# Seven instead of four SwiGLU pairs computed by seven products, in a Conformer / RG-LRU block on one core

## The chip, the cores and the metric

The kernel runs on one core of a Trainium2 chip. Five engines work side by side and meet through semaphores: TensorE (PE in the profile, with its weight loads as PEld), VectorE (DVE), ScalarE (ACT), GpSimd (POOL) and SyncE (SP), which here issues every DMA transfer. The metric is the time of one execution on the device, in microseconds (us); lower is better. All inputs and the output are float32, and the matmuls take them as pairs of fp32r parts, a high part and the low part that is left over.

## What is computed

The block has a token mixer (a causal Conformer convolution beside an RG-LRU recurrence, merged by gates), then a SwiGLU channel mixer, with a residual and an RMSNorm around each. Sequence 512, width 1024, channel mixer 2816 wide. The change sits in the channel mixer:

```python
def reference(x, norm1_g, w_in, ...):
    ...
    m = jax.nn.sigmoid(z_ga) * y_a + jax.nn.sigmoid(z_gb) * y_b
    x = x + m @ w_mix_out[l]

    h = rmsnorm(x, norm2_g[l])
    x = x + (jax.nn.silu(h @ ffn_w1[l]) * (h @ ffn_w3[l])) @ ffn_w2[l]
    return rmsnorm(x, norm_f_g)
```

## The kernel before

**Stages.** By their matmuls in the trace: the way in (`z`, `g`: 0 to 325 us), the two ways out of the token mixers (`yb` with the chunks `lo`, 325 to 380; `ya` with the chunks `co`, 380 to 423), the mixers' merged product (`mxr`, to 463), the SwiGLU products (`f` and `fr`, 463 to 700) and the last product with `ffn_w2` (`or`, 700 to 803).

**Products.** Every product is three matmuls: high by high, high by low, low by high. A SwiGLU *pair* is the two tiles k and k + 11 of 128 hidden columns each (KF = 11 pairs); the plain form (`mm3`, L432, called at L1063 and L1064) takes 2 tiles x 2 weights x 8 blocks x 3 = 96 matmuls of 512 columns. A pair in `SEVEN` (L44) goes through `ffn_seven` (L1011): seven quarter products, Strassen's scheme in Winograd's form, of 2 x 4 x 3 = 24 matmuls of 256 columns each, 168 in all, with sums of the inputs (`f_inputs`, L990, made once) and of the weights. Plain before: pairs 0, 1 and 6 to 10; seven products: 2 to 5.

**Sums of weights for the SwiGLU pairs.** `make_f_sums` (L315) is a generator; `next(f_sums_steps, None)` runs one step of it per entry of `ORDER` (64 entries, L764) and per tile of `yb` (8, L791). Each pair has four pieces. A piece loads 2 x 256 KB into a tile of the pool `wsums` (3 tiles, L87), two steps later does four additions on GpSimd (L342 to L345), and five weight chunks after that stores 512 KB (L349) to DRAM, from where the chunks `ft..` fetch it again. A piece starts every third step, from step 4.

**Weight chunks.** `weights(key)` (L161) emits the chunks up to four ahead. A chunk takes a tile of the pool `raws` (4 tiles, L85) and one DMA of 512 KB or two of 256 KB, then a tile of `hls` (5 tiles, L86): ScalarE copies the high part (L117) and VectorE, or GpSimd in the way in, subtracts for the low part (L118). A plain pair has four chunks (`raw_f`), a pair of seven products has seven (three `raw_fb`, four `raw_ft`). The last product has chunks of two quarters, in the order b21_0, b11_0, b11_1, b21_2, b11_2, b11_3, b21_4, ... (L249 to L255); b11_k also holds t1 of k and is used from step k on, b21_k serves steps k and k + 1.

**Sums of the weights of the last product.** `out_sums(n)` (L959) makes the next n of eleven: `make_sums` (L276) takes two `raws` tiles, loads 512 KB into each (L279), does four VectorE operations, and stores 4 x 256 KB (L289) to DRAM. The code calls it behind each pair: 2 behind a plain pair, `k % 2` behind one of seven products, and whatever is left behind pair 10 (L1066). Before, this gives 2, 0, 1, 0, 1, 2, 2, 2, and 1 behind pair 9: none is left behind pair 10.

**Sums of a pair's results.** `Sevenfold.pair` (L825) makes the operands of the last product from a finished pair's tiles: 6 VectorE operations (one of 0.69 us, five of 0.42) and two ScalarE casts. It is called as soon as the pair is done (L823, L1054). It leaves five of the 63 `long` tiles (L32) in use per pair until the last product.

**Order.** Instructions of one engine run in order. A scheduler fixes that order when the kernel is built: of the instructions that could go, the earliest in the program first; an instruction that needs a pool tile goes when one is free. `tc.issue_after` adds lower bounds only.

Of the kernel before, what the change touches and what calls it, by code (L numbers as in the profile page):

```python
# [9 lines left out]
F32R = mybir.dt.float32r  # L10
# [3 lines left out]
P = 128  # L14
T = 512
# [25 lines left out]

SEVEN = (2, 3, 4, 5)  # L44
SUMS_AT, SUMS_STEP, SUMS_LAG, STORE_LAG = 4, 3, 2, 5


# [33 lines left out]
def tile_block(ctx, tc, a, out):  # L81
    nc = tc.nc
    pool = lambda name, bufs, **k: ctx.enter_context(tc.tile_pool(name=name, bufs=bufs, **k))
    consts = pool("consts", 1)
    raws = pool("raws", RAW)  # L85
    hls = pool("hls", HL)  # L86
    wsums = pool("wsums", 3)  # L87
    psum = pool("psum", 6, space=bass.MemoryType.PSUM)
    psum2 = pool("psum2", 2, space=bass.MemoryType.PSUM)

# [6 lines left out]
    def pairt(name, dtype=F32R):  # L97

        return longt(f"{name}h", dtype), longt(f"{name}l", dtype)
# [7 lines left out]
    vec, act, pe, pool_e = nc.vector, nc.scalar, nc.tensor, nc.gpsimd  # L107
# [4 lines left out]
    def sub(eng, o, x, y):  # L112
        return eng.tensor_tensor(out=o, in0=x, in1=y, op=ALU.subtract)  # L113

    def split_to(h, l, full, eng, copy=act.copy):

        copy(h, full)  # L117
        last = sub(eng, l, full, h.bitcast(F32))  # L118
        if eng is pool_e:
            newest["sub"] = last.ins  # L120
        return h, l

    def split(name, full, eng, p_=None, copy=act.copy):
        p_ = p_ or pairt(name)
        return split_to(*p_, full, eng, copy)
# [4 lines left out]
    emitted = [0]  # L130
# [70 lines left out]
    ORDER = """u0 u1 rx0 rx1 gb0 rx2 u2 g0 rx3 gb1 g1 u3 rx4 g2 gb2 r0 r1 u4 g3 rx5 rg0 g4 rx6 rg1 u5 r2 r3 g5 rx7  # L201
        gb3 rg2 rx8 g6 rg3 u6 r4 r5 rx9 g7 gb4 rg4 u7 g8 r6 r7 rg5 gb5 g9 rg6 gb6 r8 r9 rg7 gb7 ga0 rg8 ga1 rg9
        ga2 ga3 ga4 ga5 ga6 ga7""".split()
    ORDER = [(t.rstrip("0123456789"), int(t.lstrip("abcdefghijklmnopqrstuvwxyz"))) for t in ORDER]
# [92 lines left out]
    F_SUMS = ("t2", "t1", "t4", "t3")  # L297
    f_sums = {k: dram.tile([P, 4, 1024], F32, tag=f"fs{k}", name=f"fs{k}") for k in SEVEN}

# [15 lines left out]
    def make_f_sums():  # L315

        todo = [(k, i, c) for k in SEVEN for i in range(2) for c in (0, 2)]
        sums_due, stores_due = [], []  # L320
        n = 0
        while todo or sums_due or stores_due:
            if stores_due and emitted[0] >= stores_due[0][0]:
                stores_due.pop(0)[1]()
            if sums_due and n >= sums_due[0][0]:
                sums_due.pop(0)[1]()
            if todo and n >= SUMS_AT and (n - SUMS_AT) % SUMS_STEP == 0:
                k, i, c = todo.pop(0)
                raw = wsums.tile([P, 1024], F32, tag="wsum", name=f"fws{k}_{i}_{c}")
                q = [raw[:, 256 * m : 256 * m + 256] for m in range(4)]  # L330
                four = (w1, w3)[i].rearrange("p (h k) (e n) -> p h k e n", h=2, e=2)
                with tc.issue_after(newest["load"]):
                    for h in range(2):
                        nc.sync.dma_start(
                            raw[:, h * T : h * T + T].rearrange("p (e k n) -> p e k n", e=2, k=2),
                            four[:, h, c : c + 2, :, k * P : (k + 1) * P].rearrange("p k e n -> p e k n"),
                        )

                def sums(raw=raw, q=q, k=k, at=T * i + P * c):
                    q11, q12, q21, q22 = q  # L340
                    with tc.issue_after(newest["sub"]):
                        sub(pool_e, q22, q22, q12)  # L342
                        sub(pool_e, q12, q12, q11)
                        pool_e.tensor_tensor(out=q11, in0=q22, in1=q11, op=ALU.add)
                        sub(pool_e, q21, q21, q11)  # L345

                    def stores():
                        with tc.issue_after(newest["load"]):
                            nc.sync.dma_start(f_sums[k][:, :, at : at + 256], raw.rearrange("p (m n) -> p m n", m=4))  # L349

                    stores_due.append((emitted[0] + STORE_LAG, stores))

                sums_due.append((n + SUMS_LAG, sums))
            n += 1
            yield

    for k in range(KF):
        if k in SEVEN:
            for n in ("b11", "b21", "b22", "t2", "t1", "t3", "t4"):
# [84 lines left out]
    def w_tiles(key, kt, ahead=AHEAD):  # L444
        h, l = weights(key, ahead)
        return [(h[:, k, :], l[:, k, :]) for k in range(kt)]
# [205 lines left out]
    def run_beside(n):  # L652
        for _ in range(n):
            next(side, None)
# [107 lines left out]
    f_sums_steps = make_f_sums()  # L762
# [30 lines left out]
            mixq.make_sums(j // 2 - 1)  # L793
    yb = sgb
    run_beside(1000)
    for _ in f_sums_steps:
        pass


    add = lambda o, x, y: vec.tensor_tensor(out=o, in0=x, in1=y, op=ALU.add)  # L800
# [8 lines left out]

    class Sevenfold:  # L810
        def __init__(self, q):
            self.q, self.uv, self.ops = q, [], []
            self.name, self.kh = q.name, q.kh

        def tile(self, j, make):

            k, i = j % self.kh, j // self.kh
            if i == 0:
                self.uv.append((longt(f"{self.name}u{k}"), longt(f"{self.name}v{k}")))
            for dst, cs in zip(self.uv[k], HALVES):  # L820
                make(cs, dst[:, HALVES[i]])
            if i:
                self.pair(k, *self.uv[k])  # L823

        def pair(self, k, ua, va):  # L825

            n = self.name
            u_ = split(f"{n}us{k}", ua, vec)
            s1 = shortt(f"{n}s1{k}")[:, LO]
            add(s1, va[:, LO], va[:, HI])  # L830
            sp = longt(f"{n}s1p{k}", F32R)
            split_to(sp[:, LO], sp[:, HI], s1, vec)
            e = longt(f"{n}e{k}")
            sub(vec, e[:, HI], ua[:, LO], va[:, LO])
            sub(vec, va[:, LO], s1, ua[:, LO])
            sub(vec, e[:, LO], ua[:, HI], va[:, LO])
            self.ops.append((u_, sp, e, va))
# [58 lines left out]
    for n, j in enumerate(mixq.order()):  # L896
        ws = w_tiles(f"co{j}", ND)
        ps = bank(f"ya{j}")
        mm3(ps, ws, un)
        o = sga[j]  # L900
        vec.scalar_tensor_tensor(out=o, in0=ps, scalar=pc("conv_b_out", j), in1=o, op0=ALU.add, op1=ALU.mult)
        m7.tile(j, lambda cs, dst: add(dst, o[:, cs], yb[j][:, cs]))
        if n == 0:
            mixq.make_sums(3)


    x2 = [[longt(f"x2{t}{h}") for h in range(2)] for t in range(NT)]
# [48 lines left out]
    o7 = Sevenfold(outq)  # L956
# [54 lines left out]
    def ffn_seven(k):  # L1011
        u_, v_ = longt(f"ou{k}"), longt(f"ov{k}")

        def product(ps, x_, w_, again=False):

            h, l = weights(f"f{w_}_{k}")
            for i in range(2):
                for c, (xh, xl) in enumerate(f_in[x_]):
                    for m, (lw, rx_) in enumerate(((h, xh), (h, xl), (l, xh))):
                        pe.matmul(  # L1020
                            ps[:, HALVES[i]], lw[:, 4 * i + c, :], rx_, start=not (again or i or c or m),
                            stop=bool(i and c == 3 and m == 2), skip_group_check=True,
                        )

        def out_of(c, dst):
            act.activation(c[:, LO], c[:, LO], AF.Silu)
            vec.tensor_tensor(out=dst, in0=c[:, LO], in1=c[:, HI], op=ALU.mult)

        r1, r2, r3, r5, r7 = bank(f"fr1_{k}"), bank2(f"fr2_{k}"), bank(f"fr3_{k}"), bank2(f"fr5_{k}"), bank(f"fr7_{k}")
        product(r1, "a11", "b11")  # L1030
        c11 = shortt(f"c11_{k}")
        act.copy(c11, r1)
        product(r2, "a12", "b21")
        add(c11, r2, c11)
        out_of(c11, u_[:, LO])
        product(r3, "s4", "b22")
        product(r1, "s2", "t2", True)
        q = shortt(f"q_{k}")
        act.copy(q, r1)
        product(r5, "s1", "t1")  # L1040
        add(q, r5, q)
        c12 = shortt(f"c12_{k}")
        add(c12, r3, q)
        out_of(c12, u_[:, HI])
        product(r7, "s3", "t3")
        c21 = shortt(f"c21_{k}")
        act.copy(c21, r7)
        add(q, r7, q)
        out_of(q, v_[:, HI])
        product(r1, "a22", "t4", True)  # L1050
        add(c21, r1, c21)
        out_of(c21, v_[:, LO])
        o7.uv.append((u_, v_))
        o7.pair(k, u_, v_)  # L1054

    for k in range(1, KF):
        if k in SEVEN:
            ffn_seven(k)
            out_sums(k % 2)
            continue  # L1060
        for j in (k, k + KF):
            p1, p3 = bank(f"f1_{j}"), bank(f"f3_{j}")
            mm3(p1, w_tiles(f"f1_{j}", ND), h2)  # L1063
            mm3(p3, w_tiles(f"f3_{j}", ND), h2)  # L1064
            ffn_out(j, p1, p3)
        out_sums(2 if k < KF - 1 else KF)  # L1066
# [96 lines left out]
```

## Time and profile before

| What | us |
|---|---|
| time, median of 3 runs (lowest, highest) | 814.71 (814.35, 815.43) |
| profiled execution: its time | 814.89 |
| profiled execution: span from first to last instruction | 813.0 |
| DVE busy | 644.1 (79%) |
| ACT busy | 443.1 (55%) |
| POOL busy | 210.3 (26%), nothing between 304 and 476 us |
| one piece of SwiGLU weight sums on POOL (fws) | 4 x 0.74 to 0.76 |
| one sum for the last product on DVE (ows) | 4 x 0.69 |

The profile comes from one execution. Its span is shorter than the time by 1.9 us, which lie around the instructions. A line of the timeline reads: start, duration, engine and line of the code, operation, what it writes and reads, how many merged into this line, and in brackets the idle time before it and what ended that. A line of the windows reads: the stretch, its length, the busy time of each engine with its number of instructions, the granted TensorE clock, the mean busy share of the 16 DMA engines, and what they moved in GB/s.

### The profile page before, as it was taken

The page shows a single profiled execution, that of the slowest core. Times are in us where ns is not written, and L with a number is a line of the kernel's source. Part 1 is how long each engine was busy: PE and PEld are TensorE (multiplying, and loading weights), DVE is VectorE, ACT ScalarE, POOL GpSimd, SP SyncE. Part 2 cuts the span into 40 slices and gives each one's busy share as a digit, 9 for nine tenths or more (in the row PEclk, how much of TensorE's full clock was granted, in tenths as well). Part 3 has the DMA queues.
Part 4 walks back from the last instruction along what each step waited for, and adds up shares of the span by engine and source line. Part 5 has one row for each costly group of instructions (what it writes and reads, how often), then busy time and mean ns, then how long its engine had stood idle before and what let it go on. Part 6 is the DMA issues. An engine that isn't in the chain of part 4 may idle for free.

```text
span 813.0 us, 11453 instructions
## 1 busy us (share of the span) xinstructions
PE 800.0 (98%) x4038; PEld 683.3 (84%) x4038; DVE 644.1 (79%) x1010; ACT 443.1 (55%) x626; POOL 210.3 (26%) x156
## 2 busy tenths in 40 slices
PE   8999999999999999999999999999999999999996
PEld 7988888888887888888888898999988888888884
DVE  4699899998999987777878769797875664688456
ACT  7546688776687755653336554364632223476442
POOL 3565768766675740000000042000000000000000
PEclk9999999999999999999999999999999999999998
DMA  6646475666654522358638535788778778576542
GB/s 209 193 123 171 136 202 176 189 193 198 186 170 130 182 75 65 116 171 263 217 104 259 156 97 176 238 262 248 224 247 282 249 271 297 177 250 216 169 160 104
DMA packets 182029, 153.46 MB, mean 189 GB/s; under 512 B 12519, under 2 KB 150163, under 8 KB 181971
## 3 DMA queue, kind: packets, MB, share of 16 engines
q1 hardware_dynamic: 181971, 152.72, 60.7%
q8 instruction: 32, 0.52, 0.3%
q14 instruction: 26, 0.21, 0.1%
HBM read 123.46 MB, written 26.21 MB: 184 GB/s over the span
## 4 chain that ended last, share of the span: by engine, by line
PE 93%; DVE 4%; issue 1%; DMA 1%; SPq 0%; POOL 0%; ACT 0%; POOLq 0%
PE z L441 31%; PE f L441 19%; PE or L844 13%; PE fr L1020 10%; PE yb L441 7%; PE ya L441 5%; PE mxr L844 5%; DVE cv L600 2%; PE g L721 2%; DMA raw_in<-in_w_in_dram 1%; PE th L481 0%; DVE xb L745 0%; PE tx L481 0%; DVE of L1086 0%; SPq L397 0%
## 5 line engine op out<-in xcount | busy, mean ns | idle before, releaser
L600 DVE SCALAR_TENSOR_TENSOR cv<-u,par,cv 128x511 f32<-128x511 f32 (+17 forms) x240 | 162.6, 729 | 1.1 <-ACT cv L597 0.9
L113 POOL TENSOR_TENSOR hl_in<-raw_in,hl_in 128x1024 fp32r<-128x1024 f32 x52 | 125.5, 2418 | 94.0 <-ACT hl_in L117 92.0
L117 ACT CAST hl_in<-raw_in 128x1024 fp32r<-128x1024 f32 x52 | 54.3, 1044 | 5.9 <-PE z L441 3.0
L117 ACT CAST hl_f<-raw_f 128x1024 fp32r<-128x1024 f32 x28 | 29.3, 1050 | 49.1 <-DMA raw_f<-in_ffn_w_dram 36.0
L113 DVE TENSOR_TENSOR hl_ob<-raw_ob,hl_ob 128x1024 fp32r<-128x1024 f32 (+1 forms) x23 | 27.1, 1178 | 26.8 <-ACT hl_ob L117 26.6
L113 DVE TENSOR_TENSOR hl_f<-raw_f,hl_f 128x1024 fp32r<-128x1024 f32 x28 | 36.2, 1304 | 14.3 <-ACT hl_f L117 14.2
L994 POOL TENSOR_TENSOR hf<-h20h,h20l 128x512 f32<-128x512 f32 x1 | 1.3, 1287 | 171.8 <-DVE h20l L485 171.8
L117 ACT CAST hl_ob<-raw_ob 128x1024 fp32r<-128x1024 f32 (+1 forms) x23 | 23.4, 1015 | 40.3 <-PE or L844 17.4
L441 PE MATMUL z<-h10h,hl_in 128*128 128x512 f32 (+1 forms) x112 | 42.4, 380 | 2.7 <-DVE h10l L485 1.5
L441 PE MATMUL z<-h15h,hl_in 128*128 128x512 f32 (+1 forms) x112 | 42.0, 376 | 0.0
L441 PE MATMUL z<-h16h,hl_in 128*128 128x512 f32 (+1 forms) x112 | 42.0, 376 | 0.0
L441 PE MATMUL z<-h17h,hl_in 128*128 128x512 f32 (+1 forms) x112 | 41.9, 376 | 0.0
L441 PE MATMUL z<-h11h,hl_in 128*128 128x512 f32 (+1 forms) x112 | 41.8, 375 | 0.0
L441 PE MATMUL z<-h12h,hl_in 128*128 128x512 f32 (+1 forms) x112 | 41.8, 375 | 0.0
L441 PE MATMUL z<-h14h,hl_in 128*128 128x512 f32 (+1 forms) x112 | 41.8, 375 | 0.0
L441 PE MATMUL z<-h13h,hl_in 128*128 128x512 f32 (+1 forms) x112 | 41.8, 375 | 0.0
L113 POOL TENSOR_TENSOR fws<-fws 128x256 f32<-128x256 f32 x48 | 36.3, 756 | 2.3
L113 DVE TENSOR_TENSOR ows<-ows,ows 128x512 f32<-128x512 f32 x22 | 15.2, 689 | 20.6 <-DMA ows<-in_ffn_w_dram 20.4
L113 DVE TENSOR_TENSOR hl_ot<-raw_ot,hl_ot 128x1024 fp32r<-128x1024 f32 (+1 forms) x17 | 20.1, 1191 | 11.1 <-ACT hl_ot L117 10.7
L441 PEld LDWEIGHTS z<-h10h,hl_in 128*128 128x128 f32 x112 | 21.3, 191 | 7.4 <-DVE h10l L485 1.8
L117 ACT CAST hl_ot<-raw_ot 128x1024 fp32r<-128x1024 f32 (+1 forms) x17 | 17.5, 1028 | 16.5 <-PE or L844 14.8
L441 PEld LDWEIGHTS z<-h15h,hl_in 128*128 128x128 f32 x112 | 21.4, 191 | 3.8
(905 smaller groups left out, 2574.9 us busy)
## 6 DMA issues: line engine op xcount, KB each, us to landing
raw_in<-in_w_in_dram SPq DMA_DIRECT2D x52, 512.0 KB
raw_f<-in_ffn_w_dram SPq DMA_DIRECT2D x28, 512.0 KB
ows<-in_ffn_w_dram SPq DMA_DIRECT2D x22, 512.0 KB
ot<-ows SPq DMA_DIRECT2D x44, 256.0 KB
raw_ob<-in_ffn_w_dram SPq DMA_DIRECT2D x33, 256.0 KB
raw_ot<-ot SPq DMA_DIRECT2D x33, 256.0 KB
fws<-in_ffn_w_dram SPq DMA_DIRECT2D x32, 256.0 KB
fs<-fws SPq DMA_DIRECT2D x16, 512.0 KB
```

Of the source, the lines that this page charges most:

```text
L113: return eng.tensor_tensor(out=o, in0=x, in1=y, op=ALU.subtract)
L117: copy(h, full)
L441: pe.matmul(ps, l, r, start=i == 0, stop=i == n - 1)
L600: vec.scalar_tensor_tensor(out=acc[c][:, s:], in0=u[c][:, : T - s], scalar=dw(c, s), in1=acc[c][:, s:], op0=ALU.mult, op1=ALU.add)
L721: pe.matmul(ps, l, r, start=k == 0, stop=k == len(mms) - 1)
L844: pe.matmul(banks[i], l_[:, ts], r_, start=start and n == 0, stop=stop and n == 2, skip_group_check=again)
L994: pool_e.tensor_tensor(out=v, in0=h2p[c][0].bitcast(F32), in1=h2p[c][1].bitcast(F32), op=ALU.add)
L1020: pe.matmul(ps[:, HALVES[i]], lw[:, 4 * i + c, :], rx_, start=not (again or i or c or m), stop=bool(i and c == 3 and m == 2), skip_group_c ...
```

## The change

It puts pairs 2 to 8 instead of 2 to 5 through seven products, so that 28 instead of 16 pieces of weight sums are made. Pieces start every third step up to step 64 and every second step after; the eight tiles of `ya` now run steps too, and what is left is run behind them. With nothing else due, stores no longer wait for five chunks. A finished pair is put on a list (`waiting`); `release` makes its sums. In a pair of seven products the list is released in its middle, ahead of its sixth product, except for the newest `max(0, k - 6)` pairs: pair 6 waits through pair 7, pairs 6 and 7 through pair 8, and all three are released at the head of pair 9, which is plain. The high and low parts of `us` of pairs 0 to 2 are put into tiles of `wsums` (six `long` tiles less). The calls of `out_sums` are unchanged, and give, from pair 1 on: 2, 0, 1, 0, 1, 0, 1, 0, 2, and 4 behind pair 10.

```diff
-SEVEN = (2, 3, 4, 5)
+PIECES = 3
+SEVEN = (2, 3, 4, 5, 6, 7, 8)
...
-    wsums = pool("wsums", 3)
+    wsums = pool("wsums", PIECES)
...
-        n = 0
+        n, next_at = 0, SUMS_AT
         while todo or sums_due or stores_due:
-            if stores_due and emitted[0] >= stores_due[0][0]:
+            if stores_due and (emitted[0] >= stores_due[0][0] or not (todo or sums_due)):
                 stores_due.pop(0)[1]()
             if sums_due and n >= sums_due[0][0]:
                 sums_due.pop(0)[1]()
-            if todo and n >= SUMS_AT and (n - SUMS_AT) % SUMS_STEP == 0:
+            if todo and n >= next_at:
+                next_at += SUMS_STEP if n < len(ORDER) else SUMS_STEP - 1
                 k, i, c = todo.pop(0)
...
     run_beside(1000)
-    for _ in f_sums_steps:
-        pass
...
             if i:
-                self.pair(k, *self.uv[k])
+                self.waiting.append((k, *self.uv[k]))
+                self.release()
+
+        def release(self, keep=0):
+
+            while len(self.waiting) > keep:
+                self.pair(*self.waiting.pop(0))
 
         def pair(self, k, ua, va):
 
             n = self.name
-            u_ = split(f"{n}us{k}", ua, vec)
+
+            p_ = None
+            if n == "o" and k < PIECES:
+                both = wsums.tile([P, 1024], F32R, tag="wsum", name=f"{n}us{k}")
+                p_ = both[:, :T], both[:, T:]
+            u_ = split(f"{n}us{k}", ua, vec, p_)
...
         if n == 0:
             mixq.make_sums(3)
+        next(f_sums_steps, None)
+
+    for _ in f_sums_steps:
+        pass
...
         out_of(c12, u_[:, HI])
+
+        o7.release(max(0, k - 6))
         product(r7, "s3", "t3")
...
         o7.uv.append((u_, v_))
-        o7.pair(k, u_, v_)
+        o7.waiting.append((k, u_, v_))
 
     for k in range(1, KF):
         if k in SEVEN:
             ffn_seven(k)
             out_sums(k % 2)
             continue
+        o7.release()
         for j in (k, k + KF):
```

More of the change, by code (lines that the diff above doesn't have):

```diff
@@ L811, in __init__ @@
         def __init__(self, q):
-            self.q, self.uv, self.ops = q, [], []
+            self.q, self.uv, self.ops, self.waiting = q, [], [], []
             self.name, self.kh = q.name, q.kh
```

## The prediction

> **What bounds the kernel now.** I read the page's busy times first, then the chain of waits, then the stages as windows, then the DMA issues of SP. The busy times and the chain, merged by line:
>
> ```profile
> PE 800.0 (98%) x4038; PEld 683.3 (84%) x4038; DVE 644.1 (79%) x1010; ACT 443.1 (55%) x626; POOL 210.3 (26%) x156
> ...
> 510.94 80.63 PE fr L1020 x672
> 591.57 108.83 PE f L441 x480
> 700.40 102.93 PE or L844 x453
> ```
>
> TensorE is the bound, and in these three stages without a gap. So only fewer or shorter matmuls gain, and anything that starves PE there costs in full. The stretch of 80.63 us is four pairs by seven products, 20.16 us each; that of 108.83 us is five plain pairs, 21.77 us each. A 256-column matmul takes 80.63 / 672 = 0.120 us, slightly more than half of a plain one's 108.83 / 480 = 0.227.
>
> The windows (the two ways out, one pair by seven products, two plain pairs, the start of the last product):
>
> ```profile
> 314.00:380.00 66.00, 66.00 (x292) 54.64 (x291) 51.36 (x73) 36.53 (x55) 0.00 (x0) 1.00 0.48 152
> 380.00:423.50 43.50, 43.50 (x193) 36.05 (x192) 33.71 (x58) 14.02 (x18) 0.00 (x0) 1.00 0.58 184
> ...
> 531.10:551.30 20.20, 20.20 (x170) 20.20 (x170) 17.71 (x27) 12.91 (x20) 0.00 (x0) 1.00 0.82 249
> ...
> 656.90:678.60 21.70, 21.70 (x97) 17.96 (x97) 12.80 (x22) 6.12 (x8) 0.00 (x0) 1.00 0.85 279
> 678.60:700.40 21.80, 21.80 (x98) 18.06 (x97) 10.61 (x17) 6.01 (x8) 0.00 (x0) 1.00 0.61 212
> 700.40:725.00 24.60, 24.60 (x110) 20.36 (x110) 19.74 (x28) 16.42 (x23) 0.00 (x0) 1.00 0.75 266
> ```
>
> DVE and DMA, not POOL, are what has little left: DVE 17.7 of 20.2 us in a pair by seven products, DMA 279 GB/s at a share of 0.85 in a plain pair with two sums for the last product. The granted clock is 1.00 throughout.
>
> Last, SP's transfers around the plain pairs:
>
> ```profile
> 599.29 1.01 SPq L144 DMA_DIRECT2D raw_f<-in_ffn_w_dram  x2
> 600.40 5.51 SPq L279 DMA_DIRECT2D ows<-in_ffn_w_dram  x3
> 608.27 2.50 SPq L289 DMA_DIRECT2D ot<-ows  x4
> 611.58 0.33 SPq L279 DMA_DIRECT2D ows<-in_ffn_w_dram  x1
> 612.01 1.01 SPq L144 DMA_DIRECT2D raw_f<-in_ffn_w_dram  x2
> 615.98 5.07 SPq L289 DMA_DIRECT2D ot<-ows  x4
> 621.89 1.01 SPq L144 DMA_DIRECT2D raw_f<-in_ffn_w_dram  x2
> 623.00 5.47 SPq L279 DMA_DIRECT2D ows<-in_ffn_w_dram  x3
> ...
> 703.72 3.70 SPq L1076 DMA_DIRECT2D x2b<-x2k  x8
> ```
>
> The order is the program's: the four chunks of the next pair, then the two sums (four loads) of this one, then four chunks again. Nothing later overtakes, since all of them want one of the four `raws` tiles. A sum keeps its two tiles from its load to the landing of its stores: first load at 600.4, next load in a freed tile at 611.6, so 11.2 us, two sums at a time.
>
> **The change, part by part.**
>
> *Three pairs by seven products.* 288 matmuls at 0.227 go, 504 at 0.120 come: 3 x (21.77 - 20.16) = 4.8 us less on PE. This is all there is to win.
>
> *Their chunks and VectorE work.* Seven instead of four 512 KB chunks per pair. Over seven pairs that is 7 x 3.67 MB + 3 sums x 2.10 MB = 32.0 MB in 141.1 us, 227 GB/s, against (4 x 3.67 + 2 x 2.10) / 80.63 = 234 before; the same for DVE, as a sum falls on every second pair as now. PE had no gap there. 0 us, between 0 and 3 (a gap of about 1 us a new pair if a chunk were late).
>
> *Pairs' sums in the middle of the next pair.* The same 2.8 us of DVE (0.69 + 5 x 0.42) and two casts on ACT, moved behind another operation; needed only by the last product. Queued behind them on DVE are the seven products' own additions, whose banks PE wants back a pair later. 0 us; without that cover 2.8 us for each of four pairs. Pairs 6 to 8 come at the head of pair 9: 3 x 2.8 = 8.4 us on a DVE that has 21.8 - 12.8 = 9.0 us idle there. It fits just; it can delay the sums below by some us.
>
> *Twelve more pieces of weight sums.* 12 x 4 x 0.74 = 36 us on POOL, which idles from 304 to 476 us, and 12 x 1.05 MB of transfers; four pieces fall before step 64, the others into the ways out. There 8 x 1.05 = 8.4 MB over 109.5 us raise 165 GB/s (mean of the two windows) to 241, under the 279 shown. On SP, chunks of `lo` and `co` stand behind a store that waits for POOL; `hl_co` is ready some 15 us ahead of PE (third chunk cast at 380.6 for a use at 396.2). 0 us, at most 2 (below).
>
> *The `us` parts in `wsums`, stores not waiting.* Pool bookkeeping; 0 us: the pieces' tiles are free long before pair 0 ends at 490 us. A late store would hold pair 0's sums, wanted only at the last product, 200 us later.
>
> *Four sums behind pair 10.* Here the calls of `out_sums` give 2, 0, 1, 0, 1, 0, 1, 0, 2 and 4, so eight loads of 512 KB stand behind the chunks b21_0, b11_0, b11_1, b21_2 and ahead of b11_2. New times: pair 9 begins at 510.9 + 7 x 20.16 = 652.0, pair 10 at 673.8, the last product at 695.6, and its step 2, which opens with b11_2, 2 x 4.08 us later (steps begin at 700.2 and 704.3 in the matmuls' rows), at 703.7. The four sums begin where the second plain pair's did, 623.0 - 591.6 = 31.4 us after the first plain pair begins: 683.4. Four raw tiles, two sums at a time: 683.4 + 2 x 11.2 = 705.8 is when b11_2 can be loaded. From load to the end of the split a chunk takes 6.3 us (load 599.3, cast 603.2, subtraction to 605.6): ready at 712.1, **8.4 us late**. Lower end: from the buffers alone, were all `raws` and `hls` kept full, the sums' loads start some 1.4 us earlier: 7.0. Upper end, by transfers: three sums and the loads of the fourth are 7.34 MB, at 279 GB/s 26.3 us, chunk ready at 683.4 + 26.3 + 6.3 = 716.0, 12.3 late; if the eight `x2b` and the two `gf` transfers (2.62 MB, 9.4 us) also go ahead of it, 21.7. They went 3.3 us into this stage before, so some of them may. I take the middle of 8.4 and 12.3, **10.4 us**, as tile turnover and transfers are both near their limits in these rows; later chunks come after it in the same order and are not later still.
>
> On this term the Trainium skill, in DMA: Bandwidth & Descriptors (Bandwidth), has 341 GB/s for a 1 MB transfer into SBUF from another issuer; by it the 7.34 MB take an estimated 21.5 us, turnover would bind alone, and the sum would have 8.4 in place of 10.4. No slice of this trace moves more than 282.
>
> **Sum.** -4.8 + 10.4 = +5.6 us: span 813.0 + 5.6 = 818.6; on the median of the runs (0.2 below the profiled 814.89) 814.7 + 5.6 = **820.3**.
>
> **The rivals.**
>
> *Not slower: the sums are out of the way in time.* If b11_2 is loaded by 697.4 (703.7 - 6.3), all of the 4.8 stays: 809.9. For it: chunks are loaded 20 us and more ahead in the plain stretch, and with no sums behind pairs 6 and 8 by seven products the queue may run further ahead than I reckon. Against it: the queue's lead is capped by 4 + 5 tiles, and chunks b11_1 and b21_2 themselves hold `raws` tiles until PE frees `hls`. It decides at a load of b11_2 at 702.2, where the stall equals the gain. Chance 0.20.
>
> *Stall about equal to the gain*, 3 to 6.4 us: 813 to 816.3. Chance 0.06.
>
> *The residual's reload goes first* and its 9.4 us come on top: 21.7 late, 814.7 - 4.8 + 21.7 = 831.6. For it: `long` tiles are freed earlier than before (six fewer used), and these loads need no `raws` tile. Against: part of them overlaps the turnover's idle transfers. Chance 0.10.
>
> *GpSimd slows VectorE in the ways out*, with no late stall. This pair of rows shows it; the first subtraction takes 2.23 us beside GpSimd's additions, against a median of 1.22:
>
> ```profile
> 483.06 2.23 DVE L113 TENSOR_TENSOR hl_f<-raw_f,hl_f 128x1024 fp32r<-128x1024 f32 x1
> ...
> 481.95 2.27 POOL L994 TENSOR_TENSOR hf<-h25h,h25l 128x512 f32<-128x512 f32 x1
> ```
>
> If each of 16 POOL operations held DVE for its 0.74 us in `ya`'s 43.5 us, that were 11.8 us against 9.8 idle: 2 us late, 809.9 + 2 = 811.9. Against: the first chunks' 15 us of lead. The Trainium skill, SBUF — State Buffer, has the two engines take a shared port pair as an exclusive lock for a whole instruction; the two rows agree. Chance 0.04.
>
> *Forecast*: 0.60, own range 816.9 (7.0 late) to 822.2 (12.3 late), with b11_3 and b21_4 late by a little more up to 826.
>
> **How the numbers follow.** Faster or slower means by more than 0.2%, 1.6 us, about what a measurement of this kernel can tell from no change. Slower: 0.60 + 0.10 and nearly none of the second rival: 0.70. Faster: 0.20 + 0.04, less 0.01: 0.23. Same: 0.07. The range has to reach over the not-slower case: 809.5 to 826.0; it leaves out the reload case and little else.
>
> **What would show it.** Right: `fr` with 1176 matmuls in 141 us without a gap, 192 `f` matmuls in 43.5 us, and then, within 10 us of the last product's start, PE idle some 10 us, released by the subtraction of `hl_ob`, with SP showing eight `ows` loads between the loads of b21_2 and b11_2, the last of them near 700. POOL busy to about 440 us. Wrong: no idle PE behind the first two steps of `or` (then the order or the lead was misread, and about 810 comes out), or gaps in `fr` or `ya` instead.

## The result: slower by 2.4%, and the profile after

The changed kernel takes 833.91 us (median of 4 runs, 833.16 to 835.55) against 814.53 us of the kernel before on the same chip (813.86 to 815.43): a ratio of 1.0243, interval 1.0227 to 1.0258 (ratios compare all runs, not the two medians, so they differ a little from the medians' quotient). The forecast was 820.3, its range 809.5 to 826.0. The profiled execution took 835.55 us, its span 833.8, so the spans differ by 20.8 us.

The page's busy times and queue, then the same queue before (its columns: packets, MB moved, share of the time of 16 DMA engines):

```profile
PE 801.6 (96%) x4254; PEld 692.2 (83%) x4254; DVE 674.8 (81%) x1034; ACT 458.3 (55%) x650; POOL 252.2 (30%) x204
...
q1 hardware_dynamic: 199731, 170.03, 66.0%
```

```profile
q1 hardware_dynamic: 181971, 152.72, 60.7%
```

PE is busy about as long as before (801.6 against 800.0 us), although 4.8 us of matmuls are gone: some of its matmuls became slower. The change moves 17.3 MB more: 12 pieces of 1.05 MB, and three more chunks of 0.52 MB for each of three pairs.

Where the 20.8 us are, by the first and last matmuls of each stage:

| Term, by the forecast's names | forecast, us | measured, us |
|---|---|---|
| three pairs by seven products | -4.8 | -4.8 (first `fr` to first `or`: 189.5, now 184.7) |
| chunks, VectorE work and moved sums in these pairs | 0 | 0 |
| twelve more pieces of weight sums (start of `fr`) | 0, at most 2 | +2.2 (510.8, now 513.0) |
| four sums behind pair 10, wait for b11_2 | +10.4 (7.0 to 12.3) | +11.1 |
| later chunks | 0 | +7.1, wait for b21_4 |
| matmuls at a lower granted clock behind these waits | not named | +5.6 |
| the end | 0 | -0.4 |
| sum | +5.6 | +20.8 |

The three terms around `or` make 23.8 us: 103.1 us before, 126.9 now, from its first matmul to the end of the 453rd of its 462, where the chain of waits leaves PE. The windows after (the second way out; the mixers' product; all pairs by seven products; two plain pairs; the starved stretch of the last product), in the columns of before:

```profile
380.00:423.50 43.50, 43.50 (x194) 36.03 (x193) 39.82 (x59) 15.51 (x20) 11.91 (x13) 1.00 0.87 271
423.50:463.00 39.50, 37.72 (x168) 30.37 (x167) 34.72 (x56) 20.69 (x35) 3.11 (x4) 1.00 0.85 270
513.00:654.10 141.10, 141.10 (x1178) 141.10 (x1177) 109.60 (x159) 74.50 (x107) 0.00 (x0) 1.00 0.77 240
654.10:697.60 43.50, 43.50 (x194) 36.02 (x193) 30.54 (x55) 15.80 (x24) 0.00 (x0) 1.00 0.68 222
705.00:736.00 31.00, 12.76 (x44) 9.00 (x43) 17.60 (x28) 9.87 (x15) 0.00 (x0) 0.74 0.91 321
```

The seven pairs run without a gap, 141.1 us of 141.1. The second way out, where some of the pieces went, rose from 184 to 271 GB/s without a gap; PE lost 1.8 us in the mixers' product behind it. That product takes 42.6 us from its first matmul to the first of `f`, against 39.9 before; it began 0.5 earlier, which leaves the 2.2 of the table. In 705 to 736 PE works 12.8 of 31 us while the transfers run at 321 GB/s, share 0.91: the stage waits for data.

PE's waits in the last product (total us, times, longest), and its timeline around the two gaps:

```profile
PE or L855 <- ACT hl_ob L118: 18.2, 2, 11.1
```

```profile
719.76 1.22 PE L855 MATMUL or<-hl_ob,ous 128*128 128x512 f32 x2 [11.11 <-ACT hl_ob L118]
...
734.43 2.91 PE L855 MATMUL or<-hl_ob,ous4h 128*128 128x512 f32 x5 [7.09 <-ACT hl_ob L118]
...
739.27 0.63 PE L855 MATMUL or<-hl_ob,ous4h 128*128 128x512 f32 x1
739.70 0.63 PE L855 MATMUL or<-hl_ob,ous4l 128*128 128x512 f32 x1
...
742.22 0.39 PE L855 MATMUL or<-hl_ob,ous5l 128*128 128x512 f32 x1
742.45 0.62 PE L855 MATMUL or<-hl_ob,ous5h 128*128 128x512 f32 x2
```

Two gaps, both ended by the cast of a chunk of `ffn_w2`: step 2 waits for b11_2, step 4 for b21_4. Behind the second a matmul starts every 0.43 us (739.27, 739.70), later every 0.23 (742.22, 742.45).

What SP sends in that time:

```profile
686.27 0.81 SPq L243 DMA_DIRECT2D raw_ob<-in_ffn_w_dram  x2
687.17 5.62 SPq L280 DMA_DIRECT2D ows<-in_ffn_w_dram  x3
...
699.47 1.33 SPq L280 DMA_DIRECT2D ows<-in_ffn_w_dram  x3
...
709.00 0.38 SPq L280 DMA_DIRECT2D ows<-in_ffn_w_dram  x1
...
712.08 0.45 SPq L280 DMA_DIRECT2D ows<-in_ffn_w_dram  x1
714.43 0.33 SPq L243 DMA_DIRECT2D raw_ob<-in_ffn_w_dram  x1
...
720.74 4.04 SPq L1094 DMA_DIRECT2D x2b<-x2k  x8
...
726.42 1.95 SPq L243 DMA_DIRECT2D raw_ob<-in_ffn_w_dram  x3
```

The eight loads of the four sums (3 + 3 + 1 + 1) stand between b21_2 and b11_2, whose first transfer goes at 714.43. Then come the rest of b11_2 and b11_3, the last sum's stores, and at 720.74 the residual's reload, eight `x2b` and two `gf`; b21_4 goes only behind them, at 726.42. The chain of waits tells the same story (start, duration, what):

```profile
712.08 4.94 DMA ows<-in_ffn_w_dram
...
722.50 4.51 DMA x2b<-x2k
727.03 6.23 DMA raw_ob<-in_ffn_w_dram
733.34 1.05 ACT hl_ob L118
734.43 1.22 PE or L855 x2
```

The start of step 4 hangs on a load of the last sum, then on the reload, then on b21_4's own 6.2 us.

### The profile page after: what moved, and what is told of

It reads as the page before. It is cut to its first block, busy times and chain, and to the rows that moved or that the text cites. A ratio compares the mean times of both kernels' runs of the same rounds, so it can differ in the third digit from the quotient of the medians.

```text
span 833.8 us, 12084 instructions
## 1 busy us (share of the span) xinstructions
PE 801.6 (96%) x4254; PEld 692.2 (83%) x4254; DVE 674.8 (81%) x1034; ACT 458.3 (55%) x650; POOL 252.2 (30%) x204
## 5 line engine op out<-in xcount | busy, mean ns | idle before, releaser
L114 POOL TENSOR_TENSOR fws<-fws 128x256 f32<-128x256 f32 x84 | 68.4, 816 | 90.9 <-DMA fws<-in_ffn_w_dram 87.1
L114 DVE TENSOR_TENSOR hl_ft<-raw_ft,hl_ft 128x1024 fp32r<-128x1024 f32 x28 | 34.1, 1219 | 10.9 <-ACT hl_ft L118 10.9
L114 DVE TENSOR_TENSOR hl_ob<-raw_ob,hl_ob 128x1024 fp32r<-128x1024 f32 (+1 forms) x23 | 27.1, 1176 | 19.3 <-ACT hl_ob L118 19.0
L1035 PE MATMUL fr<-hs_0h,hl_ft 128*128 128x256 f32 x224 | 41.5, 283 | 0.0
L118 ACT CAST hl_ft<-raw_ft 128x1024 fp32r<-128x1024 f32 x28 | 29.1, 1048 | 21.5 <-DMA raw_ft<-fs 21.5
L114 DVE TENSOR_TENSOR hl_fb<-raw_fb,hl_fb 128x1024 fp32r<-128x1024 f32 x21 | 26.8, 1274 | 10.8 <-ACT hl_fb L118 10.7
L1035 PEld LDWEIGHTS fr<-hs_0h,hl_ft 128*128 128x128 f32 x224 | 35.5, 192 | 0.0
L1035 PE MATMUL fr<-hs_0l,hl_ft 128*128 128x256 f32 x112 | 31.7, 283 | 0.0
L118 ACT CAST hl_fb<-raw_fb 128x1024 fp32r<-128x1024 f32 x21 | 22.0, 1048 | 17.5 <-DMA raw_fb<-in_ffn_w_dram 8.9
```

The costliest lines, as they stand in the source:

```text
L1035: pe.matmul(ps[:, HALVES[i]], lw[:, 4 * i + c, :], rx_, start=not (again or i or c or m), stop=bool(i and c == 3 and m == 2), skip_group_c ...
```

## The experiments

The theory: the loss is the four sums left behind pair 10, which hold back b11_2 by tile turnover and transfers, and the reload, which holds back b21_4. Rivals: the lower clock behind the gaps is a cause of its own; another part of the change costs the time; or the sums' transfers cost it wherever they stand. Edits are against the changed kernel. Each kernel was timed beside the kernel before, whose median was 814.1 to 814.4 in all of them. "Pairs" is the time from the first `fr` matmul to the first `or` (before 189.5, after 184.7), "`or`" that from its first matmul to its 453rd (before 103.1, after 126.9). Both are read from one profiled execution of each kernel.

### One sum behind each pair of seven products, none left behind pair 10

```diff
-            out_sums(k % 2)
+            out_sums(1)
```

> The changed kernel, but one sum for the last product behind every one of the seven pairs by seven products (now k % 2), so 2 + 7 + 2 = 11 and none is left behind pair 10. Theory (the four sums behind pair 10 make the whole loss of the last product, 23.8 us from its first matmul to its last): the idle of TensorE at the last product's steps 2 and 4 (11.1 and 7.1 us) and the low clock there go, that stage is back at 103 us, and the span is 833.8 - 23.8 = 810.0, the time some 812. Rival (the stage starves because transfers as such are at their limit, wherever the sums stand): the seven pairs now move 7 x (3.67 + 2.10) MB in 141 us, 286 GB/s, which is more than the 279 of a plain pair; then gaps open in the pairs, several us, and the time stays above 816.

829.34 us (828.33 to 830.63), ratio 1.0187 (1.0171 to 1.0203); `or` 103.1, pairs 202.6. The end of its chain, its waits and the window of the seven pairs:

```profile
715.92 102.95 PE or L855 x453
```

```profile
PE fr L1035 <- ACT c L1047: 6.8, 4, 2.7
```

```profile
512.00:672.00 160.00, 149.86 (x1181) 147.95 (x1180) 118.01 (x175) 74.15 (x106) 0.00 (x0) 0.96 0.82 254
```

The last product is whole again, 102.95 us as before: all 23.8 us of its loss come from the sums behind pair 10 and what they push back. But the pairs are 17.9 us longer, and the time is only 4.6 below the changed kernel's. PE waits there for copies that free its banks (`c`), which stand on ACT behind casts of late chunks. The theory is right on the place, the third rival on the price. That the transfers' rate is the limit there is not shown: 254 GB/s at a share of 0.82 is less than the 279 at 0.85 that a plain pair had without a gap, and what the sums take of the raw tiles and of VectorE was not tried apart.

### The residual's reload at step 6 instead of step 0

```diff
-                if k == 0:
+                if k == (6 if n == "o" else 0):
                     begun()
```

> The changed kernel, but the reload of the residual (eight transfers of 256 KB, with two for the norm's weight) is asked for behind step 6 of the last product instead of step 0. Theory (the second gap, 7.1 us before step 4, is the price of the reload, which SP issues at 720.7 to 726.1 ahead of chunk b21_4): the second gap shrinks to below 2 us and the first stays at about 11; the time falls by 5 to 9 us to about 826. Rival (b21_4 is late because the sums still hold the raw tiles): the second gap stays at 5 us or more and the time moves by less than 3.

828.94 us (828.18 to 830.85), ratio 1.0185 (1.0168 to 1.0201); pairs 184.7, `or` 121.0. The waits of the last product:

```profile
PE or L855 <- ACT hl_ob L118: 13.8, 2, 12.5
```

The second gap falls from 7.1 to 1.3 us and the time by 5.0; the first gap stays (12.5). So the reload is what held b21_4, and it had no part in b11_2.

### Matmuls that fill the gaps

Extra matmuls into a bank that nothing reads, ahead of steps 2 and 4; in a second version 56 and 18 of them.

```diff
+                if n == "o" and k in (2, 4):
+                    fill = bank2(f"fill{k}")
+                    for _ in range({2: 48, 4: 30}[k]):
+                        pe.matmul(fill, onesr, self.ops[0][0][0], start=True, stop=True)
```

> The changed kernel with 48 extra matmuls of 512 columns (10.9 us) ahead of step 2 of the last product and 30 (6.8 us) ahead of step 4, into a bank that nobody reads, so that TensorE is busy in the two gaps. Theory (of the stage's 23.8 us about 18.2 are idle and 5.6 the matmuls behind a gap, which run at half the granted clock: 0.43 us each instead of 0.23): the granted clock stays at 1.00, the chunks come no earlier, and the time falls by 4 to 6 us to about 829. Rival (the clock costs nothing, the stage waits for its chunks anyway): within 1.5 us of 833.9.

836.63 us (834.57 to 838.75), ratio 1.0276 (1.025 to 1.0301); `or` 126.6. The second fill ran 3.2 us past its chunk, so the sizes were changed:

> The changed kernel with extra matmuls into a bank that nobody reads, fitted to the two gaps: 56 (12.7 us) ahead of step 2 of the last product, 18 (4.1 us) ahead of step 4; the first trial had 30 there, which ended 3.2 us behind the chunk. Theory (the matmuls behind a gap run at half the granted clock and make 5.6 of the stage's 23.8 us): 3 to 5 us under the changed kernel's 833.9. Rival (the fill costs what it saves): 833 or more.

836.05 us (834.3 to 837.57), ratio 1.0266 (1.0248 to 1.0284); `or` 127.2. The timeline of the second version at step 4:

```profile
738.09 1.88 PE L855 MATMUL or<-hl_ob,ous4h 128*128 128x512 f32 x4 [2.91 <-ACT hl_ob L118]
```

Nothing is gained by keeping PE busy. In part the fill cost what it saved: 12 matmuls (2.7 us) that had run ahead of the first gap now come behind it, and step 4 starts at 738.1 instead of 734.4. Of these 3.7 us, 1.9 are there at the stage's start (699.5, was 697.6), from the mixers' product; why the chunk came another 1.8 later was not followed up. What the slower clock alone costs was therefore not isolated; that it follows the gaps is seen, that it costs the 5.6 us is the remainder of a sum.

### Four pairs by seven products, all other edits kept

```diff
-SEVEN = (2, 3, 4, 5, 6, 7, 8)
+SEVEN = (2, 3, 4, 5)
```

> The changed kernel with four pairs by seven products (2 to 5) again; all the rest stays: pairs' sums in the middle of the next pair, parts of the first three pairs in the pool of the weight sums, stores that need not wait. Sixteen pieces of weight sums, all begun before step 52, and none of the sums for the last product left behind pair 10. Theory (these moves cost nothing by themselves): 814.5, within 1.0. Rival (moving the pairs' sums or the pool costs TensorE time in the SwiGLU products): 816 or more.

814.27 us (813.7 to 815.06), ratio 1.0001 (0.9991 to 1.001). Its chain:

```profile
510.34 80.63 PE fr L1035 x672
590.98 108.83 PE f L443 x480
699.80 102.97 PE or L855 x453
```

The three lengths of before to 0.04 us. The moved pairs' sums, the parts in `wsums` and the new steps of the generator cost nothing by themselves. Not in this run are the longer wait of pairs 6 to 8 and the twelve more pieces.

### Five and six pairs

Pairs 2 to 6 leave one sum behind pair 10, pairs 2 to 7 two.

```diff
-SEVEN = (2, 3, 4, 5, 6, 7, 8)
+SEVEN = (2, 3, 4, 5, 6)
```

> The changed kernel with five pairs by seven products (2 to 6): 20 pieces of weight sums, all begun by step 61, none in the second way out; one sum for the last product is left behind pair 10. Theory (a pair by seven products gains 1.6 us; each sum left behind pair 10 takes two raw tiles for some 11 us and 2.1 MB from a stretch that has little room, and one of them fits into the lead): no gap in the last product, 814.3 - 1.6 = 812.7. Rival (the loss comes from the pairs by seven products themselves or from the pieces): not under 814.3.

814.68 us (813.42 to 819.8), ratio 1.0019 (0.9999 to 1.0039); pairs 187.9, `or` 107.8. The gap in its last product, and VectorE ahead of it:

```profile
704.85 1.39 PE L855 MATMUL or<-hl_ob,os1p 128*128 128x512 f32 x3 [2.83 <-DVE ov L985]
```

```profile
700.04 0.69 DVE L114 TENSOR_TENSOR ows<-ows,ows 128x512 f32<-128x512 f32 x1 [2.72 <-DMA ows<-in_ffn_w_dram]
...
704.29 0.41 DVE L985 TENSOR_TENSOR ov<-si,f 128x256 f32<-128x256 f32 x1
```

This gap is of another kind. VectorE runs in order; a late sum's subtraction stood at its head until the load had landed (2.72 us idle), and `ov`, the last pair's result, stood behind it, with the bank that PE wanted. The theory (no gap, 812.7) missed. The profiled execution took 816.98, 2.3 more than the median, so the median run loses less here than this trace shows.

```diff
-SEVEN = (2, 3, 4, 5, 6, 7, 8)
+SEVEN = (2, 3, 4, 5, 6, 7)
```

> The changed kernel with six pairs by seven products (2 to 7): 24 pieces of weight sums; two sums for the last product are left behind pair 10. Theory: PE gains 3.2 us; two sums take one turn of the raw tiles (11.2 us) in place of two, which is about the lead that the chunks have, so the last product stalls by 0 to 3 us: 811 to 814. Rival (the loss is in proportion to the sums left, 23.8 / 4 each): 12 us of loss and 823.

819.19 us (818.18 to 821.84), ratio 1.0064 (1.0041 to 1.0088); pairs 186.3, `or` 111.7. It lies between the theory (811 to 814) and the rival (823). With 0, 1, 2 and 4 sums left, the last product takes 103.1, 107.8, 111.7 and 126.9 us, and the pairs 189.5, 187.9, 186.3 and 184.7. The gain of 1.6 us a pair is there each time, and each sum left costs 4 to 8 us in these traces. By the medians the first costs less: five pairs gain 1.6 and end at 814.68 beside 814.36 of before, so some 2 us.

### The sums moved ahead of the pairs

Two of them behind the first two pairs, so that two instead of four are left:

```diff
         ffn_out(j, *pf[i])
+    out_sums(2)
```

> The changed kernel with two of the sums for the last product made behind pair 0, where DMA moves 85 to 180 GB/s; seven pairs by seven products, two sums left behind pair 10. Theory (what counts is where the transfers have room): the loss of the last product falls from 23.8 us to 0 to 5; VectorE there is at 21.7 of 22.8 us, so up to 3 us may be lost before pair 2: 812 to 818. Rival: the sums starve the first pair by seven products and the stall of the last product stays: over 825.

825.27 us (823.96 to 826.62), ratio 1.0134 (1.0114 to 1.0154); pairs 190.7 (+6.0), `or` 109.8. The theory (812 to 818) missed: 6.7 us of the last product's loss stay, and the pairs lose in the first of the seven what the rival said, in gaps of up to 0.8 us between 519 and 536. Four of them between the tiles of `yb`, so that none is left:

```diff
+        if j in (0, 1, 3, 5):
+            outq.make_sums((0, 1, 3, 5).index(j))
...
-    sums_of = iter(range(KF))
+    sums_of = iter(range(4, KF))
```

> The changed kernel with four of the sums for the last product made in the first way out (beside its tiles 0, 1, 3 and 5), where DMA moves 203 GB/s and VectorE is busy for 50 of 66 us; the others as called, so that none is left behind pair 10. Theory: no gap in the last product (103 us), the seven pairs unchanged, so the span falls by 23.8 us, less what four times 2.75 us of VectorE and 8.4 MB cost in the ways out, which have 16 us and about 75 GB/s of room: 810 to 814. Rival (transfers are at their limit from 350 us on, so the loss only moves): gaps of several us in the second way out or the mixers' product, 816 or more.

833.71 us (832.88 to 835.21), ratio 1.024 (1.022 to 1.0259). Its chain and a window of the ways out:

```profile
536.65 141.11 PE fr L1037 x1176
...
721.32 102.96 PE or L857 x453
```

```profile
380.00:423.50 43.50, 41.63 (x165) 32.91 (x165) 31.76 (x48) 11.99 (x16) 7.70 (x8) 0.92 0.92 282
```

Pairs and last product are as good as they can be, 184.7 and 103.1 us, but `fr` starts at 536.7 instead of 513.0: nearly all of the loss has moved into the ways out and the mixers' product, as the rival said. Transfers run at 282 GB/s, share 0.92, in this window.

### Five and six pairs with the sums spread so that none is left

```diff
-SEVEN = (2, 3, 4, 5, 6, 7, 8)
+SEVEN = (2, 3, 4, 5, 6)
...
-            out_sums(k % 2)
+            out_sums(1 if k in (3, 5, 6) else 0)
```

> The changed kernel with five pairs by seven products (2 to 6) and one more sum for the last product behind pair 6, so that none is left behind pair 10. Theory (the one sum left behind pair 10 cost some 2 us in the version with five pairs: its first subtraction waits for its loads at the head of VectorE's queue, and the last tiles of pair 10, whose banks TensorE wants, stand behind it): no wait at the start of the last product, 814.3 - 1.6 = 812.7. Rival (the extra sum only moves the loss in front of the plain pairs): 814 or more.

814.72 us (811.55 to 821.7, 12 runs), ratio 1.001 (0.9989 to 1.003); pairs 187.9, `or` 104.6. The first gap shrinks to 0.56 us, but the median is the rival's (814 or more), not the theory's 812.7.

```diff
-SEVEN = (2, 3, 4, 5, 6, 7, 8)
+SEVEN = (2, 3, 4, 5, 6, 7)
...
-            out_sums(k % 2)
+            out_sums(1 if k > 2 else 0)
```

> The changed kernel with six pairs by seven products (2 to 7) and one sum for the last product behind each of pairs 3 to 7 (2 behind pairs 1, 8 and 9), so that none is left behind pair 10. Theory (what the kernel loses is where transfers come too thick: five pairs in a row at 286 GB/s against the 279 that a plain pair moves at a share of 0.85): the last product takes 103 us again, but gaps of 3 to 8 us come in pairs 5 to 7; 814 to 820. Rival (the lead that the chunks have built up by pair 3 covers five such pairs): 811.1.

820.83 us (819.32 to 823.11), ratio 1.008 (1.0065 to 1.0094); pairs 193.6, `or` 108.0. The gaps in the pairs came as the theory said (7.4 us more than the 186.3 of six pairs); that the last product would be whole did not. Two more variants of five pairs. One has `out_sums(k % 2)` again and one sum behind the first two pairs:

```diff
         ffn_out(j, *pf[i])
+    out_sums(1)
```

> The changed kernel with five pairs by seven products (2 to 6) and the one extra sum for the last product behind pair 0 (not behind pair 6), so that none is left behind pair 10. Theory (transfers near their limit from pair 7 to the last product cause the wide spread of the version with five pairs, 811.6 to 821.7; before pair 2 they have room): the spread narrows to about 2 us and the median is 812.7. Rival (pairs by seven products with a sum behind pairs 0 and 1 begin short of lead, as the version with two sums behind pair 0 did): a gap in pair 2 and 814 or more.

816.75 us (815.34 to 817.59, 7 runs), ratio 1.0029 (1.0018 to 1.004); pairs 192.0, `or` 103.1. This is the rival: a gap of 2.64 us in pair 2, and 814 or more.

The other has the sums spread, and the reload late:

```diff
-                if k == 0:
+                if k == (6 if n == "o" else 0):
```

> Five pairs by seven products with the extra sum behind pair 6, and the reload of the residual behind step 6 of the last product in place of step 0. Theory (the spread comes from the start of the last product, where the reload's 2.6 MB stand ahead of chunk b21_4): no run over 816, median 812.5. Rival (it comes from the plain pairs ahead of it, whose sums' loads hold up VectorE's queue): spread and median stay, 814.7.

816.23 us (813.45 to 820.11, 12 runs), ratio 1.0021 (1.0008 to 1.0035); pairs 187.8, `or` 107.3. Five pairs spread are level with before, and nothing beats it. Single runs of five pairs lie 6 to 10 us apart where those of before lie within 2.4, and neither variant explains that (the late reload's theory, no run over 816, fell): with the later reload they still lie 6.7 apart, and the earlier sum narrowed it to 2.3 but cost 4.1 us in the pairs. Its cause stays open.

### A fifth tile for raw chunks

```diff
-SLOTS, SHORT = 63, 5
-RAW = 4
+SLOTS, SHORT = 61, 5
+RAW = 5
```

> The changed kernel with five instead of four raw tiles (and 61 instead of 63 long tiles, for the room). Theory (in the last product's first 40 us the transfers themselves are at their limit, 316 to 324 GB/s at a share of 0.90 and more, so another tile lets no chunk arrive earlier): the first gap stays at 9 us or more and the time within 4 us of 833.9. Rival (the turnover of the raw tiles is the limit, as the prediction reckoned its lower end): the sums and the chunks run a quarter faster, the first gap falls to 6 us or less, 827 or less.

831.03 us (828.78 to 832.25), ratio 1.0202 (1.0186 to 1.0218); pairs 188.4, `or` 119.0. Its waits and its transfers in the last product:

```profile
PE or L855 <- ACT hl_ob L118: 9.7, 2, 6.7
```

```profile
720.00:740.00 20.00, 13.30 (x45) 9.78 (x44) 10.53 (x12) 10.23 (x13) 0.00 (x0) 0.74 0.95 330
```

The first gap falls from 11.1 to 3.0 us, so tile turnover is most of it; the theory (9 us or more) fell. The rival's time (827 or less) did not come either: the second gap stays at 6.7, with transfers at 330 GB/s, share 0.95. Two `long` tiles were given up for the raw tile; the pairs are 3.8 us longer. Whether that is due to those tiles was not tried.

## Why the prediction was wrong in size

**Right.** *Three pairs by seven products* gave the 4.8 us exactly, and *Their chunks and VectorE work* and the moved pairs' sums cost nothing: 1176 matmuls without a gap, the order of the forecast, and four pairs with all other edits at a ratio of 1.0001. The direction and the place were right too: PE starves at step 2, behind the sums left after pair 10.

**The step that failed** is in *Four sums behind pair 10*: "later chunks come after it in the same order and are not later still". The order is not the same: the residual's reload stands between b11_3 and b21_4. It was weighed only as ahead of b11_2, where it would make 21.7 us, with a chance of 0.10. It went ahead of the next chunk instead and made a second gap of 7.1 us, which the forecast's own range covered only as "a little more". Moving it away took 5.8 of these 7.1. The trace of before has the same order, in the rows behind the `x2b` row that the prediction shows (b21_4 and the first half of b11_4):

```profile
708.31 0.33 SPq L1078 DMA_DIRECT2D gfh<-in_norm_f_g_dram  x1
708.98 0.33 SPq L1078 DMA_DIRECT2D gfl<-in_norm_f_g_dram  x1
709.64 1.66 SPq L242 DMA_DIRECT2D raw_ob<-in_ffn_w_dram  x3
```

The code shows it too: the reload is issued at step 0, when the chunks up to four ahead of the first two, so up to b11_3, have been asked for; b21_4 is the next.

**Terms put at nothing.** Of the 15.2 us between +5.6 and +20.8, this step makes 7.1. The slower matmuls make 5.6, the pieces 2.2, the first gap 0.7, the end -0.4. The reload alone is not the whole miss: with the second gap down to 1.3 us the time was 828.94, still above 826.0.

**The size of the first gap** came out, 11.1 us against 10.4, but by errors that cancel. The sums' loads began 10.4 us before the last product instead of 12.2 (1.8 later), the eighth load came 24.9 us behind the first instead of b11_2's after 22.4 (2.5), from it to b11_2's load passed 2.35 that were not counted, and PE could start 5.3 instead of 6.3 us after that load: 8.4 + 1.8 + 2.5 + 2.35 - 1.0 = 14.0 late, over the upper bound of 12.3. PE had 2.9 us of matmuls to run that don't use b11_2, where the forecast let step 2 open with it; 11.1 are left. The 1.0 is not a faster chunk: PE's first matmul waits for the cast alone, not for the subtraction that the 6.3 includes. Nor were there four free tiles for two sums: three loads went by 692.5, and the fourth at 699.47, when the subtraction of chunk b21_2 (at 698.23, behind the first sum's four operations on VectorE) had freed the last tile.

Of the two limits supposed, the fifth raw tile shows turnover. That transfers at 279 GB/s would bind as well is not shown. The busiest ten us of the last product before moved more, and PE lost nothing there:

```profile
708.00:718.00 10.00, 10.00 (x46) 8.29 (x45) 7.29 (x9) 6.57 (x10) 0.00 (x0) 1.00 1.02 371
```

The page's slices of 20 us hid this, with 177 and 250 GB/s there. Their highest is 297 (671 to 691), not 282, so the prediction also misread them: its upper end was worked out from too low a rate.

**Not named at all** are the 5.6 us of slower matmuls: 7.4 us at a granted clock of 0.74 and 7.4 at 0.58 make 7.4 x 0.26 + 7.4 x 0.42 = 5.0 of them:

```profile
719.80:727.20 7.40, 7.40 (x24) 5.47 (x24) 4.46 (x6) 3.89 (x7) 0.00 (x0) 0.74 0.95 316
734.40:741.80 7.40, 7.33 (x19) 5.30 (x20) 5.54 (x6) 4.98 (x6) 0.00 (x0) 0.58 0.83 292
```

***Twelve more pieces of weight sums*** cost 2.2 instead of 0, just over the bound given (2). The way named for that bound is the one that the trace shows, at other chunks: SP stands at a store that waits for GpSimd, and the next chunk of the mixers' product goes only behind it.

```profile
428.13 0.80 POOL L114 TENSOR_TENSOR fws<-fws 128x256 f32<-128x256 f32 x1
```

```profile
422.76 0.85 SPq L243 DMA_DIRECT2D raw_mxt<-mxt  x2
428.96 0.56 SPq L351 DMA_DIRECT2D fs<-fws  x1
429.62 1.56 SPq L243 DMA_DIRECT2D raw_mxt<-mxt  x2
```

Before, the loads of the chunk that here goes at 429.62 began at 415.3, and its subtraction at 431.4; now ScalarE and VectorE wait for it, and the subtraction begins at 436.5. With six pairs, whose pieces are done on GpSimd by 381, the mixers' product takes 39.8 us, as before. That this store makes the whole 2.2 us is argued from the rows; no run moved it. The bytes came more tightly than reckoned, 271 and 270 GB/s instead of the mean of 241. Beside the last piece, two VectorE operations of 0.42 took 0.99 and 0.96 us, and a subtraction 1.76 instead of 1.22. The lock of the Trainium skill (SBUF — State Buffer) cited for the rival on GpSimd and VectorE agrees with these numbers.

**The other rivals.** "Not slower" fell: b11_2 went at 714.4, not by 702.2. The reload rival had the right transfers, ahead of the wrong chunk. The 341 GB/s of the Trainium skill (DMA: Bandwidth & Descriptors, Bandwidth) were closer to this stretch's 321 than the forecast's 279; by that faster rate turnover alone would bind, 8.4, and turnover was longer than reckoned.

## What to carry to other kernels

A scheme that trades matmuls for sums of weights pays in transfers: 17.3 MB more, some 54 us at the 320 GB/s seen here, for 4.8 us of matmuls, and moving the sums only moved the place where PE waited. Before counting on hidden transfers, sum the bytes over the whole stretch in which they must go, and then list, past the first late chunk, everything that the queue sends before the next one. Look for the highest rate in short windows, too: slices of 20 us showed 177 and 250 GB/s where ten us moved 371. A stall also has a tail: count the matmuls behind it at the lower clock.

## What the runs showed of the hardware that was not expected

Gaps of PE under 3 us can already lower the granted clock. With five pairs it is 0.67 in the 5.2 us behind a gap of 2.83 us; with five pairs and the late reload 0.72 in the 6 us from a gap of 1.92 us on. Behind gaps of 0.88 and 0.76 us, in the second version with filled gaps, it stays at 1.00. The length of the gap alone does not decide: behind one of 2.26 us, with six pairs and the sums spread, the clock stays at 1.00 too (627.2 to 633.2). The Trainium skill, in TensorE: Matmul & The Clock Gate (What's actually happening), lets the clock fall to half after an idle window of some 3.4 us that runs freely and come back after as long a busy one; half rate and a tail of several us agree with 0.43 against 0.23 us a matmul until 741.8, but here idle times of 1.9 and 2.8 us could be enough.

The queue moved 321 and 330 GB/s in the starved stretches, at shares of 0.91 and 0.95, and 371 over ten us in the kernel before, where PE was never idle. So a full queue is not in itself a starved PE. What counted was which transfer stood ahead of the one that PE waited for: b21_4 went behind 2.6 MB of reload, and then took 6.2 us to land.
